# Two pairs of token-major projections by one level of Strassen's product, and x kept in device memory during attention

## The chip, the cores and the metric

The kernel runs on one core of one Trainium2 chip. The core has TensorE (PE, the matmuls; its weight loads are shown apart as PEld), VectorE (DVE), ScalarE (ACT), GpSimd (POOL) and SyncE (SP, which issues most of the DMAs). The metric is device time in microseconds (us), median of runs; a profile is one execution with its own time. Each engine takes its instructions in the order in which the program issues them, and waits on semaphores that the framework puts in.

## The reference, cut to what matters

Two layers over 512 tokens of width 1024. In each layer a normalised and modulated input h goes through one wide projection whose columns are split into thirteen parts; three kinds of attention use them.

```
h = modulate(rms_norm(x, norm1_g), shift1, scale1)
(rq, rk, rv, rg, gq, gk, gv, glr, gg, fq, fk, fv, ff) = split(h @ w_in)     # rv, rg, gv, fv: 512 columns each
ret   = silu(rg) * group_norm(retention(rq, rk, rv))
gla_o = silu(gg) * rms_norm(gla(gq, gk, gv, log_sigmoid(glr @ w_gla_a2 + b) / 16))
fox_o = forgetting_attention(rms_norm(fq), rms_norm(fk), fv, ff + b_fox_f)  # softmax, causal
mixed = sum(sigmoid(h @ w_mg + b_mg) * (branch @ w_br)) @ w_o
x     = x + gate1 * mixed
h2    = modulate(rms_norm(x, norm2_g), shift2, scale2)
x     = x + gate2 * ((silu(causal_dwconv(u)) * g) @ w_down)                 # u, g = split(h2 @ w_up)
```

All of it is float32. The matmuls use float32r, a shorter float32 form, three times: with a = a_hi + a_lo and w = w_hi + w_lo, the product is a_hi w_hi + a_hi w_lo + a_lo w_hi.

## The kernel before

**Data.** Activations are held channel-major: x as eight tiles of 128 channels by 512 tokens, h as eight pairs hhi, hlo. Tiles of 128x512 come from one pool, `slot` (59 buffers). Weights lie in device memory in *units* of 128x1024, in the order of use.

**Weights.** `dma_to` loads unit after unit on SP into a raw buffer (wr, four of them). `prep_hi` (line 118) casts it to the high part wh on ScalarE (L123), `prep_lo` (line 127) makes the low part wl = wr - wh on VectorE (L132). Five buffers hold each of wh and wl. `ahead` (line 247) prepares units up to `depth` ahead of the one in use, four during attention, and one more is loaded; `unit` hands out the next.

**Projections.** `col_block` (line 257) makes 128 output channels for all tokens: one unit, 24 matmuls with 512 columns (8 blocks of channels times three terms, L240 to L242). `tok_group` (line 523) makes a token-major output, four PSUM banks of 128 tokens by up to 512 channels: with 512 channels it takes four units and 8 x 4 x 3 = 96 matmuls (L535 to L537). There are eight PSUM banks: five for projections (`bm`) and three for the attention items (`ba`); `live` counts the latter.

**Attention items and ticks.** The attention's own work is written as generators, *items*: `qk_norm` (norms of the eight fq, fk blocks), `gates_item` and `la_item` (decays of gla and gates of fox), `fox_item` (16 blocks of softmax), `kv_item`, `gla_item`, `ret_item` (16) and, at the end of the last two, `head_out`. Each yields between stages: "e" for engine work, "p" for work that needs PSUM banks, with a condition in some. `tick` (line 205 on) admits the next item from a queue, at most eight at once, not sooner after the one before than the latter's own count of ticks (two for a norm; one, one, two, two for a head's four fox items); it moves every active item by one stage, engine stages first, then pending evacuations, then PSUM stages in order until one does not fit. A column block ticks twice, a unit of a token group twice. So the program order on every engine is a fixed interleaving of projections and items; a stage's instructions wait where they stand, with all that follows on that engine behind them.

**Order in a layer.** After the first group of fq and fk: fv, first half of gq, gk (with ff and glr, 276 columns), second half of gq, gv, four blocks of rq, four of rk, four of gg, rv, four of rg. Rotary blocks are evacuated by `rot_evac` (three VectorE instructions, L690 to L692, and a POOL add, L693). Then the three branches, fox, gla and retention: per branch eight column blocks of w_mg (L870) and four units of w_br. Then w_o, the feed-forward part and w_down, which end in x += gate * out (L907).

**x.** x is in eight buffers of its own for the whole kernel.

Of the kernel before, what the change touches and what calls it, by code (L numbers as in the profile page):

```python
# [52 lines left out]

@with_exitstack
def tile_hybrid_layers(ctx: ExitStack, tc: tile.TileContext, xT, cvec, wall, wada, par, a2, cst, tabs, out):
# [4 lines left out]
    wr_p = ctx.enter_context(tc.tile_pool(name="wr", bufs=4))  # L60
# [40 lines left out]
    crow = const.tile([1, D], F32, tag="crow", name="crow")  # L101
# [3 lines left out]
    x = [const.tile([128, S], F32, tag=f"x{k}", name=f"x{k}") for k in range(KD)]  # L105
# [3 lines left out]
    NU = wall.shape[0]  # L109

    def dma_to(u):
        while state["dma"] < min(u, NU):
            i = state["dma"]
            raw[i] = wr_p.tile([128, UW], F32, tag="wr", name="wr")
            Q.dma_start(out=raw[i], in_=wall[i])
            state["dma"] += 1

    def prep_hi(u):
        while state["prep"] < min(u, NU):
            i = state["prep"]  # L120
            dma_to(i + 1)
            hi = wh_p.tile([128, UW], F32R, tag="wh", name="wh")
            A.copy(hi, raw[i])  # L123
# [3 lines left out]
    def prep_lo(u):  # L127
        while state["lo"] < min(u, NU):
# [3 lines left out]
            V.tensor_tensor(lo, raw.pop(i), hi.bitcast(F32), op=ALU.subtract)  # L132
# [113 lines left out]

    def ahead():
        prep_to(cur[0] + depth[0])
        dma_to(cur[0] + depth[0] + 1)
# [60 lines left out]

    def h_a(l, sec, k, rb, h, ts):
        Acol = mod[l][:, (sec + 1) * 8 + k:(sec + 1) * 8 + k + 1]
        Bcol = mod[l][:, sec * 8 + k:sec * 8 + k + 1]
        t = slot("ht")
# [158 lines left out]
    def layer(l, nm, h):  # L473
# [48 lines left out]

        def tok_group(nunits, kper, width, evac):
# [20 lines left out]

        def v_evac(nm):
            def f(b, o):
                R[nm, b] = slot(nm)
                if b % 2:
                    A.copy(R[nm, b], o)
                else:  # L550
                    V.tensor_copy(R[nm, b], o)
            return f
# [188 lines left out]
        def head_out(br, hh, os, rs, mean, gain, gate):  # L741
            for b in range(NB):
# [9 lines left out]
            yield E_  # L752
            V.scalar_tensor_tensor(out=os, in0=pt, scalar=gain, in1=gate, op0=ALU.mult, op1=ALU.mult)
# [28 lines left out]
        def ret_item(hh, jb):  # L782
# [35 lines left out]
            yield ("e", 0, lambda: [("rg", hh) in R])  # L818
            yield from head_out(0, hh, os, st[:, 8:12], st[:, 0:4], der[l][:, 24 + hh:25 + hh], R["rg", hh])
# [6 lines left out]
        col_block(h, gq_evac(1))  # L826
        R["cos"], R["sin"] = slot("cos"), slot("sin")
# [382 lines left out]
```

## Time and profile before

| | |
|---|---|
| runs before | 1805.62, 1807.52, 1807.56 us; median 1807.52 |
| the profiled execution | 1807.32 us, its span 1805.5 us |
| busy over the span | PE 1796.0, PEld 1503.5, DVE 1001.8, ACT 672.4, POOL 91.0 us |
| weight units prepared (L123, L132) | 302 |
| loads of x | 8 of 256 KB, at the start |
| HBM read, written | 216.44 MB, 2.11 MB |

The span is what the trace covers; the execution's own time is 1.8 us longer. Matmuls are pipelined and their ends modelled, so a busy PE is no proof that it runs at its full pace: the pace is read from counts of matmuls in a stretch. A group's row gives line, engine, operation, tiles written and read, shape and count, then busy us, the mean ns of one, the idle time of the engine just before, and what ended it. The chain of waits is followed backwards from the last instruction: at each step to what released it.

### The profile page before, as it was taken

What the parts mean: (1) busy time and instruction counts of PE and PEld (TensorE: products, weight loads), DVE (VectorE), ACT (ScalarE), POOL (GpSimd) and SP (SyncE); (2) the same over time, 40 slices, a digit from 0 to 9 for tenths busy, and PEclk for the clock granted to TensorE, in tenths of its full rate; (3) what the DMA queues carried; (4) which work ended last, traced back from release to release, by engine and by line L of the source; (5) the groups of instructions that cost most, each with busy time, mean ns of one, the idle gap of its engine ahead of it and who ended that gap; (6) DMA issues with size and microseconds to landing.
All of it is one profiled execution on the core that took longest, in us unless ns stands there. A gap on an engine that the chain in (4) does not pass through costs nothing.

```text
span 1805.5 us, 22557 instructions
## 1 busy us (share of the span) xinstructions
PE 1796.0 (99%) x8991; PEld 1503.5 (83%) x8991; DVE 1001.8 (55%) x1515; ACT 672.4 (37%) x1124; POOL 91.0 (5%) x111
## 2 busy tenths in 40 slices
PE   9999999999999999999999999999999999999999
PEld 6888778888889888888898887888888998888887
DVE  7677654565666776664256576534444466454321
ACT  3674432332324443332138543324223244333220
POOL 3221100000000000000001010000000000000000
PEclk9999999999999999999999999999999999999999
DMA  9332233355543565554223322321322223323231
GB/s 345 120 129 70 71 104 107 129 175 185 177 140 105 183 211 200 197 187 142 81 70 116 119 71 71 117 78 63 104 93 82 82 94 118 104 94 100 70 122 48
DMA packets 64948, 220.03 MB, mean 122 GB/s; under 512 B 7320, under 2 KB 7746, under 8 KB 64843
## 3 DMA queue, kind: packets, MB, share of 16 engines
q1 hardware_dynamic: 64138, 216.47, 36.0%
q0 software_dynamic: 704, 2.11, 0.4%
q8 instruction: 71, 1.16, 0.3%
q14 instruction: 35, 0.28, 0.0%
HBM read 216.44 MB, written 2.11 MB: 121 GB/s over the span
## 4 chain that ended last, share of the span: by engine, by line
PE 93%; DVE 4%; ACT 2%; issue 1%; DMA 0%; SPq 0%; POOL 0%; DVEq 0%; ACTq 0%
PE bm L240 23%; PE bm L242 23%; PE bm L241 23%; PE bm L364 4%; PE ga L364 4%; PE bm L535 3%; PE bm L536 3%; PE bm L537 3%; PE ro L798 1%; PE rs L786 1%; DVE fl L658 1%; ACT wh L123 1%; DVE wl L132 1%; DVE fst L659 1%; DVE fl L656 0%
## 5 line engine op out<-in xcount | busy, mean ns | idle before, releaser
L132 DVE TENSOR_TENSOR wl<-wr,wh 128x1024 fp32r<-128x1024 f32 x302 | 368.7, 1223 | 308.3 <-ACT wh L123 308.0
L240 PE MATMUL bm<-hhi,wh 128*128 128x512 f32 x1296 | 520.3, 401 | 0.0
L242 PE MATMUL bm<-hhi,wl 128*128 128x512 f32 x1296 | 505.5, 390 | 0.0
L241 PE MATMUL bm<-hlo,wh 128*128 128x512 f32 x1296 | 504.9, 390 | 0.0
L123 ACT CAST wh<-wr 128x1024 fp32r<-128x1024 f32 x302 | 314.4, 1046 | 307.0 <-PE bm L241 231.9
L240 PEld LDWEIGHTS bm<-hhi,wh 128*128 128x128 f32 x1296 | 243.5, 188 | 54.2 <-issue 4.2
L241 PEld LDWEIGHTS bm<-hlo,wh 128*128 128x128 f32 x1296 | 243.6, 188 | 53.0 <-issue 2.9
L242 PEld LDWEIGHTS bm<-hhi,wl 128*128 128x128 f32 x1296 | 243.3, 188 | 52.0
L240 PE MATMUL bm<-fah,wh 128*128 128x512 f32 (+1 forms) x374 | 141.0, 377 | 0.0
L241 PE MATMUL bm<-fal,wh 128*128 128x512 f32 (+1 forms) x374 | 140.8, 377 | 0.0
L242 PE MATMUL bm<-fah,wl 128*128 128x512 f32 (+1 forms) x374 | 140.8, 376 | 0.0
L152 DVE SCALAR_TENSOR_TENSOR ar<-ar,cact 128x1024 f32<-128x1024 f32 x80 | 97.4, 1218 | 0.0
L535 PE MATMUL bm<-wh,hhi 128*128 128x512 f32 (+1 forms) x256 | 97.0, 379 | 0.0
L536 PE MATMUL bm<-wl,hhi 128*128 128x512 f32 (+1 forms) x256 | 93.5, 365 | 0.0
L537 PE MATMUL bm<-wh,hlo 128*128 128x512 f32 (+1 forms) x256 | 93.4, 365 | 0.0
L907 DVE SCALAR_TENSOR_TENSOR x<-bm,mod,x 128x512 f32<-128x512 f32 (+1 forms) x39 | 25.5, 655 | 101.3 <-PE bm L242 101.3
L241 PEld LDWEIGHTS bm<-fal,wh 128*128 128x128 f32 x374 | 70.4, 188 | 13.0
L242 PEld LDWEIGHTS bm<-fah,wl 128*128 128x128 f32 x374 | 70.4, 188 | 12.9
L240 PEld LDWEIGHTS bm<-fah,wh 128*128 128x128 f32 x374 | 70.4, 188 | 12.8
L945 DVE TENSOR_TENSOR fu<-fu,bm 128x512 f32<-128x512 f32 x42 | 28.9, 688 | 69.7 <-PE bm L242 59.8
L870 ACT ACTIVATE mg<-bm,der 128x512 f32<-128x512 f32 x48 | 32.9, 685 | 82.4 <-PE bm L242 82.4
L944 ACT ACTIVATE fu<-fu 128x512 f32<-128x512 f32 x44 | 27.8, 633 | 93.7 <-DVE fu L942 93.7
(215 smaller groups left out, 2402.0 us busy)
## 6 DMA issues: line engine op xcount, KB each, us to landing
wr<-wall SPq DMA_DIRECT2D x302, 512.0 KB, 3.5
ar<-wada SPq DMA_DIRECT2D x80, 512.0 KB, 4.0
ad<-wada SPq DMA_DIRECT2D x32, 256.0 KB, 6.1
x<-xT SPq DMA_DIRECT2D x8, 256.0 KB, 4.5
cumb<-cumd POOLq DMA_DIRECT2D x8, 256.0 KB, 4.6
dec<-tabs SPq DMA_DIRECT2D x8, 256.0 KB, 4.2
out<-x SPq DMA_DIRECT2D x8, 256.0 KB, 2.1
cos<-tabs SPq DMA_DIRECT2D x2, 256.0 KB
```

What stands on the lines that cost most here:

```text
L123: A.copy(hi, raw[i])
L132: V.tensor_tensor(lo, raw.pop(i), hi.bitcast(F32), op=ALU.subtract)
L152: V.scalar_tensor_tensor(out=r, in0=r, scalar=1.0, in1=cact, op0=ALU.mult, op1=ALU.mult, accum_out=mod[l][:, b:b + 1])
L240: T.matmul(o, lhsT=wh, rhs=ah, start=first, stop=False)
L241: T.matmul(o, lhsT=wh, rhs=al, start=False, stop=False)
L242: T.matmul(o, lhsT=wl, rhs=ah, start=False, stop=last)
L364: T.matmul(banks[f % GB][:, ts], lhsT=got[f // 8][wi][:, (f % 8) * 128:(f % 8) * 128 + 128], rhs=h[kc][hi][:, ts], start=kc == 0 and hf != ...
L535: T.matmul(o, lhsT=h[k][0][:, bs], rhs=wh[:, ws], start=k == 0, stop=False)
L536: T.matmul(o, lhsT=h[k][0][:, bs], rhs=wl[:, ws], start=False, stop=False)
L537: T.matmul(o, lhsT=h[k][1][:, bs], rhs=wh[:, ws], start=False, stop=k == KD - 1)
L870: A.activation(g, o, AF.Tanh, scale=0.5, bias=der[l][:, i * 8 + j:i * 8 + j + 1])
L945: V.tensor_tensor(t, t, pg, op=ALU.mult)
```

## The change

One level of Strassen's scheme (in Winograd's form with shared sums) is used for two products at a time that share the left operand: fv with gv, and rv with rg. The left operand is h transposed into four quarters (two halves of the tokens, two of the channels), the right one is two weights side by side, cut into the two halves of their channels. Seven products of quarters stand for eight. Sums of quarters of h (ta, tb) are made once per layer by `t_item` from the unsplit h, which `h_a` now keeps, and split into high and low parts. Sums of quarters of the weights are made for each pair on VectorE in the raw buffers, in place, before the split: `_plan` lists the 14 units that a pair prepares from its 8 raw ones, "r" for a raw one, "s" for a sum. So a pair prepares 14 units for 8, and a unit of a pair serves 12 matmuls.

rg, before made channel-major in four column blocks, comes out token-major, so retention's gate is multiplied in `head_out` ahead of the transposes. The order in the layer becomes gk, gq, gq, pair fv and gv, pair rv and rg, rq, rk, gg; fox items wait for fv. Two loops in `pair_group` run ticks alone until a condition holds. Three more units are loaded ahead instead of one, into six raw buffers.

x becomes eight tiles of the slot pool (65 buffers), which are free during attention: x is read again from device memory ahead of the third branch, in layer 1 from a copy that layer 0 writes by POOL's queue after w_down. crow becomes two tiles of the pool.

```diff
+def _plan():
+    def pair():
+        a11, a21, a22, a12 = ((b + 2 * i, b + 2 * i + 1) for i in range(4))
+        for i in range(2): v.append(("r", a11[i]))
+        for i in range(2): v.append(("s", a21[i], a21[i], a22[i], ALU.add))
+        for i in range(2): v.append(("s", a11[i], a21[i], a11[i], ALU.subtract))
+        for i in range(2): v.append(("r", a12[i]))
+        for i in range(2): v.append(("s", a12[i], a12[i], a11[i], ALU.subtract))
+        for i in range(2): v.append(("s", a11[i], a22[i], a11[i], ALU.subtract))
+        for i in range(2): v.append(("r", a22[i]))
...
-    wr_p = ctx.enter_context(tc.tile_pool(name="wr", bufs=4))
+    wr_p = ctx.enter_context(tc.tile_pool(name="wr", bufs=6))
...
-    x = [const.tile([128, S], F32, tag=f"x{k}", name=f"x{k}") for k in range(KD)]
+    x = [slot("x") for _ in range(KD)]
...
     def prep_hi(u):
         while state["prep"] < min(u, NU):
             i = state["prep"]
             dma_to(i + 1)
+            p = plan[i]
+            if p[0] == "s":
+                prep_lo(i - 1)
+                V.tensor_tensor(raw[p[1]], raw[p[2]], raw[p[3]], op=p[4])
             hi = wh_p.tile([128, UW], F32R, tag="wh", name="wh")
-            A.copy(hi, raw[i])
+            A.copy(hi, raw[p[1]])
...
     def ahead():
         prep_to(cur[0] + depth[0])
-        dma_to(cur[0] + depth[0] + 1)
+        dma_to(cur[0] + depth[0] + far[0])
...
+        def t_item(k):
+            yield E_
+            ...
+            V.tensor_tensor(ta[:, H0], c[:, H1], c[:, H0], op=ALU.subtract)
+            V.scalar_tensor_tensor(out=ta[:, H1], ...)
+            V.scalar_tensor_tensor(out=tb[:, H0], ...)
+            V.scalar_tensor_tensor(out=tb[:, H1], ...)
+            yield E_
+            A.copy(ah, ta)
+            A.copy(bh, tb)
+            yield E_
+            V.tensor_tensor(al, ta, ah.bitcast(F32), op=ALU.subtract)
+            V.tensor_tensor(bl, tb, bh.bitcast(F32), op=ALU.subtract)
+            tt[k, 1], tt[k, 2] = (ah, al, 0), (ah, al, 256)
+            tt[k, 3], tt[k, 4] = (bh, bl, 0), (bh, bl, 256)
+
+        def pair_group(done):
+            flush()
+            while live[0] > NA - 1:
+                tick()
+            ...
+            bA, bB = [bm(), bm()], [bm(), bm()]
+            o11, o12, o21, o22 = ([slot("pr"), slot("pr")] for _ in range(4))
+            def prod(banks, key, first, evac):
+                ahead()
+                us = [unit()]
+                ahead()
+                us.append(unit())
+                for t in range(2):
+                    for k in range(4):
+                        ...
+                        T.matmul(banks[t], lhsT=ah[:, ts], rhs=wh[:, ws], start=first and k == 0, stop=False, ...)
+                        T.matmul(banks[t], lhsT=ah[:, ts], rhs=wl[:, ws], start=False, stop=False, ...)
+                        T.matmul(banks[t], lhsT=al[:, ts], rhs=wh[:, ws], start=False, stop=k == 3, ...)
+                        if k == 1:
+                            tick()
+                    pend.append(lambda t=t: evac(t))
+                    tick(1, False)
+
+            prod(bA, 11, True, lambda t: A.copy(o11[t], bA[t]))
+            while len(tt) < 16:
+                tick()
+            prod(bB, 1, True, lambda t: A.copy(o22[t], bB[t]))
+            prod(bA, 2, False, lambda t: A.copy(o12[t], bA[t]))
+            while live[0] > NA - 1:
+                tick()
+            bC = [bm(), ba()]
+            ...
+            prod(bC, 21, True, e11)
+            prod(bB, 22, False, lambda t: V.tensor_tensor(o12[t], o12[t], bB[t], op=ALU.add))
+            prod(bA, 3, False, lambda t: V.tensor_tensor(o22[t], o22[t], bA[t], op=ALU.add))
+            ...
+            prod(bA, 4, False, e21)
...
-            yield ("p", 1, lambda: [("qn", hh) in R, ("qn", 4 + hh) in R, "cumb" in R])
+            yield ("p", 1, lambda: [("qn", hh) in R, ("qn", 4 + hh) in R, "cumb" in R, ("fv", NB - 1) in R])
...
                     V.tensor_scalar(o, o, mean[:, b:b + 1], rs[:, b:b + 1], op0=ALU.add, op1=ALU.mult)
+                    V.tensor_tensor(o, o, gate[b][:, hh * 128:hh * 128 + 128], op=ALU.mult)
...
-        tok_group(4, 2, 512, v_evac("fv"))
+        for k in range(4):
+            queue.append((t_item(k), 1))
+        far[0] = 3
+        tok_group(3, 3, GKW, gk_evac)
         col_block(h, gq_evac(0))
-        tok_group(3, 3, GKW, gk_evac)
         col_block(h, gq_evac(1))
+        pair_group(fg_done)
...
-        tok_group(4, 2, 512, v_evac("gv"))
+        pair_group(r_done)
+        far[0] = 1
         for i in range(4):
             col_block(h, rot_evac("rq", i))
...
-        tok_group(4, 2, 512, v_evac("rv"))
-        for i in range(4):
-            col_block(h, gate_evac("rg", i))
...
             if bi == 2:
+                for k in range(KD):
+                    x[k] = slot("x")
+                    Q.dma_start(out=x[k], in_=xT[k * 128:k * 128 + 128, :] if l == 0 else xs[k])
...
+        def upd5(j, o, ts=FULL):
+            upd5x(j, o, ts)
+            if l < L - 1:
+                ...
+                G.dma_start(out=xs[j][:, ts], in_=x[j][:, ts])
...
-NSLOT = 59
+NSLOT = 65
```

More of the change, by code (lines that the diff above doesn't have):

```diff
@@ L51, with plain @@
 NC = _o
+H0 = slice(0, S // 2)
+H1 = slice(S // 2, S)
+def _plan():
+    v, w = [], [0]
+    def plain(n):
+        for _ in range(n):
+            v.append(("r", w[0]))
+            w[0] += 1
+    def pair():
+        b = w[0]
+        a11, a21, a22, a12 = ((b + 2 * i, b + 2 * i + 1) for i in range(4))
+        for i in range(2):
+            v.append(("r", a11[i]))
+        for i in range(2):
+            v.append(("s", a21[i], a21[i], a22[i], ALU.add))
+        for i in range(2):
+            v.append(("s", a11[i], a21[i], a11[i], ALU.subtract))
+        for i in range(2):
+            v.append(("r", a12[i]))
+        for i in range(2):
+            v.append(("s", a12[i], a12[i], a11[i], ALU.subtract))
+        for i in range(2):
+            v.append(("s", a11[i], a22[i], a11[i], ALU.subtract))
+        for i in range(2):
+            v.append(("r", a22[i]))
+        w[0] += 8
+    for _ in range(L):
+        plain(8 + 3 + 2)
+        pair()
+        pair()
+        plain(12 + 36 + 8 + 6 + 2 * (KFF - 3) + KFF)
+    lim, m = [0], 0
+    for t in v:
+        m = max([m] + [i + 1 for i in t[1:4] if isinstance(i, int)])
+        lim.append(m)
+    return v, lim
 @with_exitstack
@@ L104, in tile_hybrid_layers @@
     warm = const.tile([128, S], BF16, tag="warm", name="warm")
-    x = [const.tile([128, S], F32, tag=f"x{k}", name=f"x{k}") for k in range(KD)]
+    x = [slot("x") for _ in range(KD)]
     state = {"prep": 0, "lo": 0, "dma": 0}
     raw, wgt = {}, {}
-    NU = wall.shape[0]
+    plan, wlim = _plan()
+    NU = len(plan)
     def dma_to(u):
-        while state["dma"] < min(u, NU):
+        while state["dma"] < wlim[min(u, NU)]:
             i = state["dma"]
@@ L131, in prep_lo @@
             lo = wl_p.tile([128, UW], F32R, tag="wl", name="wl")
-            V.tensor_tensor(lo, raw.pop(i), hi.bitcast(F32), op=ALU.subtract)
+            V.tensor_tensor(lo, raw[plan[i][1]], hi.bitcast(F32), op=ALU.subtract)
             wgt[i] = (hi, lo)
@@ L752, in head_out @@
             yield E_
+            if mean is not None:
+                R["br", br, hh] = split(pt, "ob", gain)
+                free()
+                return
             V.scalar_tensor_tensor(out=os, in0=pt, scalar=gain, in1=gate, op0=ALU.mult, op1=ALU.mult)
@@ L829, in layer @@
         Q.dma_start(out=R["sin"], in_=tabs[1])
-        tok_group(4, 2, 512, v_evac("gv"))
+        pair_group(r_done)
+        tt.clear()
+        far[0] = 1
         for i in range(4):
             col_block(h, rot_evac("rq", i))
-        for p in range(2):
-            for half in range(2):
-                queue.append((kv_item(p, half), 1))
         for i in range(4):
             col_block(h, rot_evac("rk", i))
+        for hh in range(NH):
+            R["dec", hh] = slot("dec")
+            Q.dma_start(out=R["dec", hh], in_=tabs[2 + hh])
+        for hh in range(NH):
+            for jb in range(NB):
+                queue.append((ret_item(hh, jb), 1))
         for i in range(4):
@@ L841, in layer @@
             queue.append((gla_item(hh), 2))
-        tok_group(4, 2, 512, v_evac("rv"))
-        for hh in range(NH):
-            R["dec", hh] = slot("dec")
-            Q.dma_start(out=R["dec", hh], in_=tabs[2 + hh])
-        for i in range(4):
-            col_block(h, gate_evac("rg", i))
-        for hh in range(NH):
-            for jb in range(NB):
-                queue.append((ret_item(hh, jb), 1))
         ada_on[0] = True
@@ L1013, in tile_hybrid_layers @@
         V.tensor_copy(onesr, ones)
-        Q.dma_start(out=crow, in_=cvec)
+        crow = [slot("crow") for _ in range(2)]
+        for i in range(2):
+            Q.dma_start(out=crow[i][0:1, :], in_=cvec[:, i * S:i * S + S])
         for k in range(KD):
@@ L1030, in tile_hybrid_layers @@
         for i in range(2):
-            T.matmul(pc[i], lhsT=ones[0:1, :], rhs=crow[0:1, i * S:i * S + S], start=True, stop=True)
+            T.matmul(pc[i], lhsT=ones[0:1, :], rhs=crow[i][0:1, :], start=True, stop=True)
         heat(W0)
```

89 lines of the change are left out of this document (70 added, 19 removed).

## The prediction

> **What bounds the kernel now.** I read the page's busy times and its chain first, then the stages, then the layer's attention stretch in order of time. Columns of a stage: stretch, its length, busy time (instructions) of PE, PEld, DVE, ACT, POOL, granted clock, DMA share, GB/s.
>
> ```profile
> PE 1796.0 (99%) x8991; PEld 1503.5 (83%) x8991; DVE 1001.8 (55%) x1515; ACT 672.4 (37%) x1124; POOL 91.0 (5%) x111
> PE 93%; DVE 4%; ACT 2%; issue 1%; DMA 0%; SPq 0%; POOL 0%; DVEq 0%; ACTq 0%
> ...
> 400.00:500.00 100.00, 100.00 (x443) 82.81 (x442) 59.78 (x82) 28.49 (x36) 0.00 (x0) 1.00 0.52 174
> ...
> 60.00:110.00 50.00, 49.98 (x262) 42.77 (x261) 34.49 (x41) 40.24 (x66) 9.06 (x7) 1.00 0.38 126
> 160.00:210.00 50.00, 50.00 (x246) 40.66 (x246) 38.59 (x65) 19.97 (x42) 7.93 (x7) 1.00 0.23 74
> ```
>
> TensorE sets the end: 93% of the chain. From 400 to 500 us it runs only 512-column matmuls, 443 in 100 us, so one costs 0.2257 us, and a unit of 24 (a column block) 5.42 us. But the same rows warn: where attention runs beside the projections, VectorE is 77% busy (160 to 210) and ScalarE 80% (60 to 110). The chain there, in order of time (start, length, what):
>
> ```profile
> 118.70 1.92 PE la L616 x8
> 130.27 0.86 PE laS L630 x4
> 131.13 0.79 PE lan L635 x8
> 158.28 0.89 PE fo L678 x8
> ...
> 168.34 0.69 DVE rt L690
> 170.73 1.30 DVE fl L658
> 172.87 0.94 ACT wh L123
> 173.83 1.22 DVE wl L132
> ...
> 207.53 0.69 DVE rt L690
> ```
>
> Between 168 and 208 us the chain leaves PE for VectorE and ScalarE. One rotary block starts each (207.53 - 168.34)/5 = 7.84 us, not 5.42. Forgetting attention's own PE work in these 2.42 us: 80 fo matmuls at 0.89/8 = 0.11 are 8.9 us, the 72 of fs and fT at about the same price 8; some 17 to 18 us over ten blocks, 1.8 a block. So 0.6 us a block, 6 us a layer, is already stall. VectorE is nearly the bound here before anything is added.
>
> **The change, part by part.** *Saved matmuls.* Per layer fv, gv, rv (96 each) and rg (four blocks of 24, 96) are 384 matmuls; two pairs of 7 products, each 2 x 4 x 3 = 24, are 336. 48 x 0.2257 = 10.8 us a layer, 21.7 in all. This stands if PE stays the bound.
>
> *What VectorE gets.* Its rows over the first layer's attention stretch, and two more shapes (line, shapes, count | busy us, mean ns | idle before, releaser):
>
> ```profile
> L132 DVE TENSOR_TENSOR wl<-wr,wh 128x1024 fp32r<-128x1024 f32 x37 | 45.0, 1220 | 23.7 <-ACT wh L123 23.6
> L467 DVE TENSOR_TENSOR qsl<-qsq,qsh 128x512 fp32r<-128x512 f32 x8 | 10.3, 1292 | 12.7 <-ACT qsh L466 12.7
> L658 DVE TENSOR_TENSOR fl<-fl,cst 128x128 f32<-128x128 f32 x16 | 9.2, 577 | 0.5
> L656 DVE SCALAR_TENSOR_TENSOR fl<-fs,cumc,cumb 128x128 f32<-128x128 f32 (+3 forms) x16 | 8.7, 542 | 5.3 <-PE fs L652 3.5 <-DMA cumb<-cumd 1.9
> L659 DVE TENSOR_REDUCE fst<-fl 128x1 f32<-128x128 f32 (+3 forms) x16 | 7.8, 487 | 0.5
> L496 DVE SCALAR_TENSOR_TENSOR qy<-qsq,qy 128x512 f32<-128x512 f32 x8 | 5.4, 679 | 0.0
> L736 DVE SCALAR_TENSOR_TENSOR st<-st,an,kv 128x128 f32<-128x128 f32 x14 | 4.9, 348 | 3.0 <-PE kv L721 2.3
> L467 DVE TENSOR_TENSOR fbl<-fo,fbh 128x512 fp32r<-128x512 f32 x4 | 2.7, 685 | 1.8 <-ACT fbh L466 1.8
> L663 DVE RECIPROCAL fst<-fst 128x1 f32<-128x1 f32 x16 | 2.5, 155 | 0.8 <-ACT fl L661 0.8
> L626 DVE TENSOR_TENSOR la<-la,lae 128x512 f32<-128x512 f32 x2 | 1.3, 671 | 0.0
> ...
> L315 DVE SCALAR_TENSOR_TENSOR ht<-x,mod,rb 128x256 f32<-128x256 f32 x16 | 7.6, 480 | 2.3 <-ACT rb L306 2.3
> ...
> L123 ACT CAST wh<-wr 128x1024 fp32r<-128x1024 f32 x37 | 38.4, 1046 | 0.0
> ```
>
> A pair loads the same 8 raw units but prepares 14: six more splits (1.22 on VectorE, 1.05 on ScalarE), and eight of them are first summed by a VectorE instruction of L132's shape, 1.22 us. A product of two summed units costs VectorE 4 x 1.22 = 4.9 us against 5.42 us of PE. And `prep_hi`/`prep_lo` issue sum, cast, low part one behind the other: the low part waits for ScalarE's cast of what VectorE has just summed, so 1.05 us more passes idle per summed unit, 7.0 us a product. Before, the cast needed nothing from VectorE and ran ahead.
>
> ```profile
> DVE wl L132 <- ACT wh L123: 308.0, 184, 5.4
> ...
> 167.01 1.23 DVE L132 TENSOR_TENSOR wl<-wr,wh 128x1024 fp32r<-128x1024 f32 x1 [1.83 <-ACT wh L123]
> ```
>
> Here VectorE stands still in front of exactly this instruction (308 us in the span, once 1.83 us under load), with its later work queued behind it. The Trainium skill ("TensorE: Matmul & The Clock Gate", on queue depths in the part on the array) has VectorE and ScalarE as strict FIFO. By that the 1.05 us are lost in full; if later instructions could pass, each layer would be 16 us cheaper than my sum. These two rows agree with the page.
>
> *Where it falls.* Work items enter one by one at ticks. Of layer 0, three gk units and two gq blocks give 2 ticks each, the first product 4: 14. Eight norms enter at every second tick, so the four t items (`t_item`) enter at ticks 17 to 20 and end at 22: the loop that waits for them runs 8 ticks with no product between. In layer 1 two blocks come first, the t items enter at 15 to 18, and 2 ticks are run so. Fox items now wait for fv, so all 16 run in pair B (24 of its 28 ticks), kv behind them. The last product accumulates into bA, which VectorE must have read one product before; so PE cannot end pair B before VectorE has come through its sixth product. VectorE's work from the start of pair A to there, layer 0: low parts of 26 units 31.7 (three of pair A's are issued earlier, one of rq comes in), 15 sums 18.3, t items 4 x (4 x 0.48 + 2 x 0.68) = 13.1, norms not yet finished, about four at 1.29 + 0.68 + 0.75 = 11, decay (6 x 0.67) and gates (seven instructions, about as much) 8, fox 30.9 less 4.6, kv 16 x 0.35 = 5.6, evacuations 12 x 0.69 = 8.3. The 4.6: L658 takes 0.29 alone and 1.30 beside POOL's rotary add, which no longer runs then:
>
> ```profile
> 130.16 0.29 DVE L658 TENSOR_TENSOR fl<-fl,cst 128x128 f32<-128x128 f32 x1
> ...
> L945 DVE TENSOR_TENSOR fu<-fu,bm 128x512 f32<-128x512 f32 x42 | 28.9, 688 | 69.7 <-PE bm L242 59.8 <-ACT fu L944 9.9
> ```
>
> (L945 is the row for an evacuation that adds.) Sum 122, and 15 waits of 1.05 make 138 us. In layer 1 two norms are left, 133. PE in the same stretch: 324 matmuls 73.1, fox 18, decay 1.92 + 2 x (0.86 + 0.79) = 5.2, gates, kv and norms 5: 101 us, 100 in layer 1. Stall: 37 and 33 us.
>
> *Bounds.* If the cast waits cost nothing, 16 a layer less. If each product takes the longer of VectorE and PE with no carry between them (low parts are issued two products ahead, 3 to 19 us of VectorE per product), it comes to 9 a layer more. I take the sum: evacuations tie the engines closely, but two products of look-ahead carry something.
>
> *Given back.* Rotary blocks without fox run at 5.42: 6 us a layer.
>
> *Edits at little or nothing.* Retention's gate is multiplied token-major: four 128-wide VectorE instructions more per head, about 4.4 us a layer, and gla's heads now share the stage of the mg blocks. VectorE there was 53% busy:
>
> ```profile
> 260.00:291.00 31.00, 31.00 (x140) 25.24 (x139) 16.56 (x24) 11.38 (x21) 1.01 (x1) 1.00 0.27 85
> ...
> x<-xT SPq DMA_DIRECT2D x8, 256.0 KB, 4.5
> wr<-wall SPq DMA_DIRECT2D x302, 512.0 KB, 3.5
> ```
>
> Some 18 us more in about 65 make 80%, where fox's stage lost 0.6 us a block: 0 to 7 a layer, I take 2. The eight reloads of x are issued on SP ahead of the third branch, twelve units (65 us) before their first reader, and land in 4.5 us; uncovered, or with the weight loads stuck behind them, 5 us a layer. The stores of x go by POOL's queue in a stage where POOL does nothing (0.00 in the row of 400 to 500). crow in two parts, tabd and the slots: 0 to 1 us, taken as 0.
>
> **The sum**, against the profiled execution's own 1807.3 us (span 1805.5; it lies 0.2 below the runs' median 1807.5): layer 0 -10.8 + 37 - 6 = +20, layer 1 -10.8 + 33 - 6 = +16, mg stages +4. 1807 + 40 = **1847 us**.
>
> **The rivals.** *PE stays the bound* (the other side). If the look-ahead of four units and VectorE's idle 45% took up the sums, the saved matmuls would be seen: 1807.3 - 21.7 = 1786, and up to 12 less for the fox stage. For it: the page's share. Against: the idle time lies in other stages. It decides itself at the row of pair A: only if a summed product costs VectorE less than 5.42 us, which with an idle cast it does not (7.0). Halfway, the casts are free and only VectorE's busy time counts: stalls 21 and 17, the sum 1847 - 32 = 1815, and with the old stalls gone entirely (9 a layer) about 1803.
>
> *The clock falls.* In the wait loops PE idles for the first time since the start. What an idle PE does, the start shows:
>
> ```profile
> 13.16 2.15 PE warm L1027 x5
> ...
> 17.03 3.07 PE warm L1027 x10
> 20.10 0.68 PE ga L364 x3
> ```
>
> 0.43 us a matmul, then 0.31, then 0.227 as work goes on, though the clock column says 1.00. Three idle stretches a layer (loop, first and sixth product of pair B), 15 matmuls each at 0.43: 3 us x 6, so 1865. At worst all of both pairs: 324 at 0.43 plus 28 is 167 against 138 and 133, some 63 more, 1910. Against it: in DVE-bound products a slow PE is partly hidden, and gaps of 1 to 3 us are short. The Trainium skill (same page, "Part 1: The HAM clock gate") lets the clock go to half after an idle window of about 3.4 us and back after a busy one; by that only the loops and pair B's first product would pay. This trace has no such gap after the start.
>
> *Raw buffers.* Six hold what eight units of a pair need; a12 is loaded only when a21 is read for the last time, and the next pair's a22 when this one's low part is made, three low parts (3.7 us) before it is summed, against 3.5 us of landing. If each of four such places were late by a landing: +14, 1861.
>
> **How the numbers follow.** My forecast, VectorE's sums bound the pairs (1815 to 1870): 0.65. PE stays the bound or nearly (1775 to 1803): 0.13. Clock or buffers (above 1860): 0.18; that gain and loss cancel (1804 to 1811), 0.04. The range from 1803 to 1878 takes in the free-cast bound and most of the clock case. 0.2%, 3.6 us, is about what a measurement can tell. Faster 0.13, same 0.04, slower 0.83.
>
> **What would show it.** Right: PE's count of 512-column matmuls down by 96; in pair A and B VectorE above 85% busy or idle only before wl on ScalarE; PE's idle time in front of the products after the t items, ending on tal or tah; the chain through wr, wl and fl; rotary blocks at 5.42. Wrong: PE back to back at 0.2257 through both pairs, or a stall that ends on wr's DMA or on SP.

## The result, and the profile after

The changed kernel takes 1911.61 us (median of 4 runs, 1910.10 to 1912.86) against 1806.64 us before (4 runs beside it, 1805.62 to 1807.56): ratio 1.058, 95% interval [1.0562, 1.0599], 105 us slower. The forecast was 1847 us with a range up to 1878: the direction is right, the size is not.

The page of the changed kernel: busy times, the chain by engine, and the two groups that prepare weight units.

```profile
span 1911.1 us, 22671 instructions
...
PE 1820.6 (95%) x8895; PEld 1506.8 (79%) x8895; DVE 1092.1 (57%) x1657; ACT 716.9 (38%) x1184; POOL 108.9 (6%) x120
...
PE 85%; DVE 7%; ACT 4%; issue 2%; DMA 0%; POOL 0%; SPq 0%; ACTq 0%; DVEq 0%; POOLq 0%
...
L179 DVE TENSOR_TENSOR wl<-wr,wh 128x1024 fp32r<-128x1024 f32 x326 | 396.7, 1222 | 314.9 <-ACT wh L170 305.7
L170 ACT CAST wh<-wr 128x1024 fp32r<-128x1024 f32 x326 | 338.8, 1047 | 437.1 <-PE bm L288 271.2
```

PE has the 96 instructions less that seven products for eight promise (8991 to 8895), and 24 more units are prepared (302 to 326). TensorE's share of the chain falls from 93% to 85%; VectorE, ScalarE and issue take it.

The stages of the changed kernel (columns as in the prediction), cut at the first matmuls of the pairs: pair A and pair B of layer 0, then of layer 1, then the stretch from the first evacuation of the mg blocks to the end.

```profile
89.70:180.30 90.60, 63.74 (x217) 46.31 (x216) 64.01 (x82) 45.20 (x70) 9.30 (x10) 0.74 0.20 64
180.30:269.30 89.00, 74.05 (x386) 55.52 (x385) 56.63 (x111) 44.91 (x91) 0.00 (x0) 0.92 0.21 65
1039.80:1122.30 82.50, 58.05 (x214) 43.76 (x213) 58.68 (x76) 38.46 (x58) 6.63 (x8) 0.81 0.21 70
1122.30:1211.30 89.00, 74.01 (x386) 55.51 (x385) 56.59 (x111) 44.91 (x91) 0.00 (x0) 0.92 0.20 65
...
1293.60:1911.00 617.40, 613.29 (x2991) 516.06 (x2989) 275.90 (x376) 198.60 (x314) 10.24 (x9) 1.00 0.28 92
```

The two pairs last 179.6 and 171.5 us; the prediction had 138 and 133. That is 42 + 38 = 80 us, more than the whole 65 us that it missed by; 15 come back elsewhere, 5 of them in the last row here (below). The amount of VectorE's work was right: 64.01 + 56.63 = 120.6 us in layer 0, against 122 predicted, and its larger terms were near too (sums 18.2 us for 18.3, fox 26.0 for 26.3). But VectorE is only 71% and 64% busy in the two pairs. It isn't full, and neither is TensorE. What fills the difference is waiting between engines, seen in the waits of layer 0's pairs (who waited for whom: us in total, times, longest):

```profile
DVE wl L179 <- ACT wh L170: 27.0, 19, 2.8
ACT wh L170 <- DVE wr L168: 20.8, 11, 2.6
...
PEld qn L541 <- ACT qsh L522: 10.6, 4, 4.6
DVE fbl L523 <- ACT fbh L522: 10.3, 2, 8.1
...
DVE qsl L523 <- ACT qsh L522: 6.7, 4, 2.5
...
DVE fst L795 <- ACT fl L793: 4.3, 6, 0.8
```

The first two rows are the ping-pong of the weight sums: the cast waits for the sum, the low part for the cast. In this view no engine waits for a weight load. The others are items: a norm (qsl, qn) and a fox block (fbl, fst). A norm's way through the engines stands in the chain of waits of the changed kernel, from the end of pair A's first product into the loop that waits for the t items (start, length, what):

```profile
99.21 0.53 ACT qsq L536
...
101.44 0.63 ACT qsq L548
102.07 0.52 ACT qsh L522
...
102.61 1.37 DVE qsl L523
...
104.03 0.81 PE qn L542
...
104.86 0.69 ACT qy L545
...
107.84 1.37 DVE qsl L523
...
112.83 1.36 DVE qsl L523
```

From ScalarE to VectorE to PE and back to ScalarE: qsl starts at 102.61, 107.84 and 112.83, one norm after another every 5.1 us. Beside the first of these two steps PE has the last six matmuls of the first product, beside the second no product at all: that loop lasts from 107.3 to 118.1 us. In the kernel before, the same instruction, five times:

```profile
L467 DVE TENSOR_TENSOR qsl<-qsq,qsh x5: 1375/1379/1385, 87.2 to 108.1; 128x512 fp32r<-128x512 f32 x5
```

(108.1 - 87.2)/4 = 5.2 us. This pace is that of the matmuls, which have no gap there (PE 49.98 of 50 us in the prediction's row from 60 to 110): one norm comes every two ticks, and two ticks of a unit with 24 matmuls held 5.42 us of them, enough to hide a norm. A product of a pair has four ticks in 5.42 us, so two ticks hold only 2.71 us. The lengths of the chain's pieces could be read in the trace of before, though not its pace.

### The profile page after: what moved, and what is told of

It is laid out like the page before. It is cut to its first block, busy times and chain, and to the rows that moved or that the text cites. A ratio compares the mean times of both kernels' runs of the same rounds, so it can differ in the third digit from the quotient of the medians.

```text
span 1911.1 us, 22671 instructions
## 1 busy us (share of the span) xinstructions
PE 1820.6 (95%) x8895; PEld 1506.8 (79%) x8895; DVE 1092.1 (57%) x1657; ACT 716.9 (38%) x1184; POOL 108.9 (6%) x120
## 4 chain that ended last, share of the span: by engine, by line
PE 85%; DVE 7%; ACT 4%; issue 2%; DMA 0%; POOL 0%; SPq 0%; ACTq 0%; DVEq 0%; POOLq 0%
PE bm L287 22%; PE bm L289 22%; PE bm L288 22%; PE bm L420 4%; PE ga L420 4%; ACT wh L170 1%; PE bm L628 1%; PE bm L632 1%; PE bm L630 1%; DVE wr L168 1%; DVE wl L179 1%; PE ro L935 1%; PE rs L923 1%; DVE fl L788 1%; PE fo L810 1%
## 5 line engine op out<-in xcount | busy, mean ns | idle before, releaser
L179 DVE TENSOR_TENSOR wl<-wr,wh 128x1024 fp32r<-128x1024 f32 x326 | 396.7, 1222 | 314.9 <-ACT wh L170 305.7
L170 ACT CAST wh<-wr 128x1024 fp32r<-128x1024 f32 x326 | 338.8, 1047 | 437.1 <-PE bm L288 271.2
L287 PE MATMUL bm<-hhi,wh 128*128 128x512 f32 x1232 | 488.5, 396 | 0.0
L289 PE MATMUL bm<-hhi,wl 128*128 128x512 f32 x1232 | 479.9, 390 | 0.0
L288 PE MATMUL bm<-hlo,wh 128*128 128x512 f32 x1232 | 479.6, 389 | 0.0
L287 PEld LDWEIGHTS bm<-hhi,wh 128*128 128x128 f32 x1232 | 231.3, 188 | 50.7 <-issue 2.9
L288 PEld LDWEIGHTS bm<-hlo,wh 128*128 128x128 f32 x1232 | 231.4, 188 | 50.1 <-issue 1.9
L288 PEld LDWEIGHTS bm<-fal,wh 128*128 128x128 f32 x374 | 70.4, 188 | 12.8
L289 PEld LDWEIGHTS bm<-fah,wl 128*128 128x128 f32 x374 | 70.4, 188 | 12.8
L287 PE MATMUL bm<-mxh,wh 128*128 128x256 f32 (+1 forms) x176 | 58.6, 333 | 0.0
L289 PE MATMUL bm<-mxh,wl 128*128 128x256 f32 (+1 forms) x176 | 58.3, 331 | 0.0
L288 PE MATMUL bm<-mxl,wh 128*128 128x256 f32 (+1 forms) x176 | 58.3, 331 | 0.0
```

What stands on the lines that cost most here:

```text
L170: A.copy(hi, raw[p[1]])
L179: V.tensor_tensor(lo, raw[plan[i][1]], hi.bitcast(F32), op=ALU.subtract)
L287: T.matmul(o, lhsT=wh, rhs=ah, start=first, stop=False)
L288: T.matmul(o, lhsT=wh, rhs=al, start=False, stop=False)
L289: T.matmul(o, lhsT=wl, rhs=ah, start=False, stop=last)
```

## The experiments

All are timed against the kernel before on the same chip. "Ratio" is to that kernel, with its 95% interval.

**Everything but the seven products** (e1_plain): the order, x in device memory, six raw buffers and token-major gates of the changed kernel, with plain token groups; no weight sums, t items or wait loops, and two ticks a unit.

```diff
-        pair()
-        pair()
+        plain(16)
...
-        pair_group(fg_done)
+        tok_group(4, 2, 512, keep("fv"))
+        tok_group(4, 2, 512, keep("gv", ...))
```

> The order of the changed kernel (gk, gq, fv, gv, rv, rg, then rq, rk, gg; rg token-major; x read again), with the plain eight products: no sums, no t items, no wait loops. If Strassen's own work on VectorE and its hand-offs cost the time, this stands near the kernel before: 1802 to 1820. If the new order alone costs it (fox held back until fv is done, norms in a bunch), 1850 or more.

Measured 1807.66 us, ratio 1.001 [0.9999, 1.0022]. The whole loss belongs to what this kernel leaves out: the products with their sums, t items, loops and ticks.

**The sums one unit early** (e2_sum_ahead): VectorE makes the next sum while ScalarE casts the last.

```diff
...
+            sum_of(i)
             A.copy(hi, raw[p[1]])
+            sum_of(i + 1)
```

> Each weight sum is issued one unit earlier, so that VectorE makes the next sum while ScalarE casts this one. VectorE's amount of work is unchanged. Theory amount (the sum of VectorE's busy time decides): no more than 5 us faster, 1906 to 1912. Theory hand-offs (VectorE stands idle behind ScalarE's cast, 1.05 us at each of 32 sums): 20 to 34 us faster, 1878 to 1892.

Measured 1880.54 us, ratio 1.041 [1.0383, 1.0444]: 31 us less. The prediction priced the cast waits at 16 us a layer, 32 in all. In the waits of layer 0's pairs VectorE's idle time in front of low parts falls from 27.0 to 17.0 us.

**No wait loop** (e3_t_first): the t items at the head of the queue.

```diff
-            queue.append((t_item(k), 1))
+            queue.insert(k, (t_item(k), 1))
```

> The four t items go to the head of the queue instead of behind the norms; VectorE does the same work, but the loop that ticks without products runs no more. Theory amount: within 8 us of the changed kernel. Theory hand-offs (in the loop the norms' chains ScalarE, VectorE, PE, ScalarE, POOL, VectorE run one after the other with nothing beside them): pair A shrinks by 20 to 35 us in layer 0 and 10 to 15 in layer 1, 1862 to 1882, and the clock stays at 1.00 there.

Measured 1910.51 us, ratio 1.058 [1.0549, 1.061]. The loop goes and nothing is gained, as was expected had VectorE's amount of work set the time. But the norms that ran in the loop now run in the products: five of their qsl start between 94.42 and 123.76 us, 5.2 to 10.5 us apart, so the products still wait for norms.

**Fox after the pairs** (e4_fox_late): fox items wait until pair B is done.

```diff
-            yield ("p", 1, lambda: [..., "cumb" in R, ("fv", NB - 1) in R])
+            yield ("p", 1, lambda: [..., "cumb" in R, "rg" in R])
```

> Fox items wait for the second pair, so they run beside the rotary blocks as before the change. If fox beside the sums is what makes pair B 89 us long: pair B 45 to 55, rotary blocks 7.5 to 8 instead of 5.4, in all 15 to 25 us a layer faster, 1862 to 1882. If pair B is bound by the sums and casts themselves: pair B stays above 65 and the time above 1890.

Measured 1889.6 us, ratio 1.046 [1.0433, 1.0494]. The stages of this run, pair A and pair B of layer 0:

```profile
87.50:173.50 86.00, 58.86 (x217) 42.74 (x216) 63.93 (x82) 45.13 (x70) 9.31 (x10) 0.78 0.20 68
173.50:213.30 39.80, 38.50 (x170) 31.44 (x169) 27.16 (x27) 19.33 (x23) 0.00 (x0) 1.00 0.43 143
```

Pair B, now almost without items, takes 39.8 us for seven products, 5.69 each, with every sum and cast wait in it and PE busy for 38.5. So sums alone don't bound a pair: with fox items in it, it took 89.0. Pair B is 49 us shorter in each layer, but the kernel only 22 us in all: fox goes back beside the rotary blocks and behind (from the first to the last evacuation of layer 0's mg blocks it is 218 us for 200).

**No sums** (e5_no_sums: the raw quarters go into the products as they are), and **half the ticks** (e6_sparse: as without the loop, and two ticks per product instead of four, the density of before), then **both cures** (e7_sparse_ahead) and **half the ticks without sums** (e15_sparse_no_sums).

```diff
 # e5, e15
-            if p[0] == "s":
-                prep_lo(i - 1)
-                V.tensor_tensor(raw[p[1]], raw[p[2]], raw[p[3]], op=p[4])
 # e6, e7, e15
-                    tick(1, False)
```

> Leaves out the 32 sums of weights (the raw quarters go into the seven products instead), all else as in the changed kernel. VectorE is rid of 32 x 1.22 = 39 us and of the waits behind the casts. Theory amount: all 39 us and the waits' 34 are seen, 1838 to 1850. Theory hand-offs: most of what the sums cost was the wait, which the run with the sums one unit earlier has gained already; little more than that run, 1865 to 1878.

> The t items at the head of the queue, and two ticks per product of a pair in place of four, so that a tick has 2.7 us of products beside it as in a column block. Same work on every engine. Theory density (an item's chain through ScalarE, VectorE, PE and POOL takes some 5 us for two ticks, whatever PE does): pair A 50 to 60, pair B 50 to 65 us, rotary blocks above 5.42 again; 1835 to 1865. Theory amount: 1900 to 1912, as the run with t items first.

> As the run with two ticks per product, and each weight sum issued one unit earlier. Theory density and hand-offs: 15 to 30 us below that run, 1812 to 1845, pair A near 45. Theory amount: no more than 5 us below it.

> Two ticks per product instead of four, and the 32 weight sums left out (their products take a cast quarter instead, so the output is not the reference's). Two ticks alone gave 1882, two ticks with the sums early 1850. If VectorE's amount of work is what is left with the sums early, leaving the sums out takes it away as well: about 1815. If what is left are the chains between engines, the time stays near that with the sums early: 1840 to 1850.

Together they make a table (us, median; ratios: 1.031 [1.0278, 1.0338] for e5, 1.041 [1.0383, 1.0443] for e6, 1.023 [1.0204, 1.0263] for e7, 1.0145 [1.0128, 1.0161] for e15):

| | sums in place | sums one unit early | no sums |
|---|---|---|---|
| four ticks a product | 1911.6 | 1880.5 | 1863.0 |
| two ticks a product | 1882.0 | 1849.6 | 1832.7 |

The second row also has the t items first, which alone was worth 1 us in the first column; in the other columns it was not run alone. The columns and rows add up: early sums are worth 31 and 32 us, the sums' own work 18 and 17, the ticks 30, 31 and 30. From 1911.6 the three take 79 us; the last cell is still 26 us above the kernel before, though 21.7 us of matmuls are gone. The ticks are worth less than was expected of them: two ticks alone were to give 1835 to 1865 us, and 1812 to 1845 with early sums. The last cell lies between the 1815 expected had VectorE's amount been what was left, and the 1840 to 1850 for the chains. The stages of the last cell and of the one left of it, pair A and pair B of layer 0 (no sums, then early sums):

```profile
94.00:148.90 54.90, 48.73 (x198) 36.88 (x197) 43.99 (x48) 42.57 (x66) 12.20 (x12) 0.94 0.28 90
148.90:211.60 62.70, 58.52 (x280) 45.33 (x279) 39.24 (x72) 36.28 (x72) 0.01 (x1) 1.00 0.30 99
```

```profile
92.90:152.60 59.70, 52.02 (x198) 38.56 (x197) 54.35 (x57) 43.02 (x66) 12.42 (x12) 0.89 0.27 85
152.60:218.50 65.90, 59.88 (x281) 46.61 (x280) 45.04 (x77) 36.29 (x72) 0.00 (x0) 0.97 0.30 99
```

With early sums VectorE is 91% busy in pair A (54.35 of 59.70): there its work is near the bound, as the prediction had it for all of both pairs.

**The density alone, in the kernel before** (e8_before_dense): four ticks per unit of a 512-wide token group instead of two (two behind each half of the unit), nothing of the change.

```diff
+                    if width == 512 and kk:
+                        tick()
...
+                        if width == 512:
+                            tick(1, False)
```

> The kernel before, with nothing of the change but four ticks per unit in the token groups of fv, gv and rv (as dense as in the pairs, twice as dense as before). Theory density: eight norms of about 5 us run against 27 us of products, so 10 us or more of stall a layer, and more where fox meets gv: 1825 to 1850, with the clock below 1.00 there. Theory amount: no change, 1803 to 1811.

Measured 1842.72 us, ratio 1.020 [1.0166, 1.0225]: 35 us lost without one sum. From 60 to 120 us PE is busy for 51.5 us, before for 60.0, and no other engine is full there (VectorE 38.5 us, ScalarE 43.5). The norms run one behind the other (VectorE's last two of eight):

```profile
96.07 1.36 DVE L467 TENSOR_TENSOR qsl<-qsq,qsh 128x512 fp32r<-128x512 f32 x1 [1.05 <-ACT qsh L466]
...
101.01 1.37 DVE L467 TENSOR_TENSOR qsl<-qsq,qsh 128x512 fp32r<-128x512 f32 x1 [2.19 <-ACT qsh L466]
```

From 71.36 us on, six steps of 4.94 us each: with 2.71 us of matmuls to two ticks, the chain sets this pace. This run and the table's rows show a cause that the prediction lacked.

**A warm TensorE** (e10_heat): the changed kernel with matmuls of no use, 12 per tick in the wait loop and one per block of channels in the first two products of each pair.

```diff
+                for _ in range(12):
+                    T.matmul(bB[0], lhsT=warm[:, 0:128], rhs=warm, start=True, stop=True)
```

> The changed kernel with matmuls put in that compute nothing (a bank that is overwritten later): 12 behind each tick of the wait loop, one behind each block of the first two products of each pair, so that PE is never idle long. Theory clock (PE at half speed in the pairs is what costs): the clock stays at 1.00 and most of the 64 us beyond the prediction come back, 1850 to 1875. Theory density: only the matmuls that ran at 0.43 us are gained, at most 17 us, less what the added ones cost, 1893 to 1912.

Measured 1909.97 us, ratio 1.057 [1.054, 1.0601]. Two stages of the changed kernel, then of this run (the column before the last two is the granted clock):

```profile
120.00:150.00 30.00, 20.19 (x65) 14.79 (x65) 23.40 (x36) 14.92 (x23) 2.94 (x5) 0.57 0.19 60
...
180.00:225.00 45.00, 35.87 (x159) 26.53 (x158) 26.41 (x56) 24.09 (x55) 0.00 (x0) 0.89 0.11 36
```

```profile
120.00:150.00 30.00, 28.19 (x130) 17.57 (x131) 23.93 (x37) 15.08 (x24) 2.94 (x5) 0.94 0.18 58
...
180.00:225.00 45.00, 36.42 (x173) 24.53 (x175) 27.57 (x58) 24.83 (x57) 0.00 (x0) 1.00 0.11 36
```

The clock rises from 0.57 to 0.94 and from 0.89 to 1.00, and VectorE gets as much done in the same time as before: the slow clock looks like a mark of the stall and not its cause. This isn't shown to the end: the added matmuls take time of PE too, so a gain of the clock that they just eat up can't be excluded.

**Other places for the items**, on top of both cures: fox held until pair B is done (e11_fox_late), the rotary query blocks ahead of pair A (e12_rq_first), and that with fox admitted from the middle of pair B (e13_rq_fox_mid).

```diff
 # e11
-            yield ("p", 1, lambda: [..., ("fv", NB - 1) in R])
+            yield ("p", 1, lambda: [..., "rg" in R])
 # e12: ahead of pair_group(fg_done)
+        for i in range(4):
+            col_block(h, rot_evac("rq", i))
```

> T items first, two ticks per product, sums one unit earlier, and fox items held until the second pair is done. Theory density: pair B about 40 us instead of 65, rotary blocks 7.5 to 8 instead of 6, fox ends later and may leave a wait ahead of its branch: 1820 to 1842 against the run without the last edit (1850). Theory amount: 1847 to 1853.

> T items first, two ticks per product, sums one unit earlier, and the four rq blocks ahead of the first pair, so that the norms have 22 us more of plain products beside them. Theory density: pair A falls from 60 to 42-48 us in both layers, the rq blocks run at 5.4 to 6; pair B as before at 60-65: 1818 to 1835. If pair A's length came from the sums and not from the norms: pair A stays above 55 and the time at 1845 or more.

> As the run with the rq blocks first, and fox items admitted only from the fourth product of pair B on, so that the rest of them falls beside rk and gg. Theory density: pair B 45 to 55 us, rk and gg blocks 7 to 8: 1805 to 1825; a gain over the kernel before (1806) only if no tick runs without products. Theory amount: as the run with the rq blocks first.

Measured 1859.4 us (1.029 [1.0261, 1.032]), 1867.2 (1.033 [1.0304, 1.0364]) and 1870.06 (1.035 [1.032, 1.038]): all above the 1849.6 they began from, where the expectations had 1805 to 1842. Fox taken from a pair is late where it goes: the mg blocks of layer 0, from the first evacuation to the last, take 218 and 221 us in the two runs that hold it back, and 200 without. With the rotary blocks first, pair A takes 63.5 us in layer 0 (42 to 48 expected); its norms still run to 148 us, and POOL's adds come beside the sums (told at the end), so it doesn't tell norms from sums.

**One pair** (e14_one_pair; its lines below are against the kernel before): the order of before, only rv and rg as a pair at rv's place, early sums, two ticks a product. Three runs then moved items around it: the t items queued ahead of gv (e18_t_early), that and gla's output items behind the pair (e17_t_early_gla_late), the same with the t items ahead of rq (e19_t_rq_gla_late). Last, the second of these with the t items at the head of the queue (e20_t_head).

```diff
-        tok_group(4, 2, 512, v_evac("rv"))
-        for i in range(4):
-            col_block(h, gate_evac("rg", i))
+        pair_group(r_done)
 # e17, e19, e20
         pair_group(r_done)
+        for hh in range(NH):
+            queue.append((gla_item(hh), 2))
 # e20, after the first rq block
+                    queue.insert(k, (t_item(k), 1))
```

> Only the pair with the values and the router gate's weights (rv with rg) by seven half products, at the place of the old value groups; queries and keys as before with four ticks of items in a unit; the weight sums one unit early, two ticks per product. The pair's seven products have about 5.4 us less of TensorE's work a layer than the eight. If the loss comes from items whose chain of engines lasts longer than the product that hides it, this pair, with few items left for it, should run near TensorE's pace: 1800 to 1812 us. If VectorE's sums are themselves the bound of a pair, the pair costs some 20 us a layer as the second pair does now: 1840 to 1850.

> The one-pair kernel (1819) with its four t items queued ahead of the value group of the second branch instead of behind the rotary query blocks, so that they are done long before the pair. In the one-pair kernel TensorE idles and runs slow for about 10 us more than before around the pair's first product (225 to 250 us of layer 0), while the state updates of the second branch wait behind the t items on VectorE. If that crowding is the loss, this gives 1799 to 1808; if the loss is the second branch's own chain, it stays at 1815 to 1820.

> As the run with early t items, and the four output items of the second branch queued behind the pair instead of ahead of it, so that nearly no item runs within the pair. If chains of items in a pair are what makes a product longer than its matmuls, the pair then runs at 5.5 us a product and the time is 1795 to 1803, below the kernel before; if the items only move their loss to the blocks behind the pair, 1806 to 1815.

> As the last, but with the t items queued just ahead of the rotary query blocks, one group later. If where the t items run doesn't matter once they are out of the way of the state updates, the same time as the last run within 4 us; if the norms of the first 100 us are crowded by early t items, this one is the faster by 4 to 8 us.

> The kernel with one pair, early t items and the second branch's output items behind the pair (1818), with its t items put at the head of the queue after the first rotary query block: in that kernel they stood behind the items of the third branch and so still ran at 221 to 234 us, where the state updates of the second branch wait behind them on VectorE. Its products 1 to 4 already take 5.4 us each, the length of their matmuls; what is left is the stretch around the first product (12.8 us instead of 5.4, and some 6 us of waits and slow matmuls ahead of it). If the t items' crowd is the cause, 1798 to 1806, at or below the kernel before (1806); if the state updates are late by themselves, 1812 to 1818.

Measured 1819.11 us (1.007 [1.0055, 1.0085]), 1817.28 (1.006 [1.0048, 1.0074]), 1818.25 (1.0065 [1.0053, 1.0078]), 1818.39 (1.006 [1.005, 1.0078]) and 1827.87 (1.011 [1.0096, 1.0132]). In the three middle runs the t items ran at about the same place as in the first, since they still stood behind the fox items in the queue: these runs tested only gla's items. The first of the five was expected at 1800 to 1812, and the one with gla's items behind the pair at 1795 to 1815: both are slower than that. The pair in the run with gla's items behind it, layer 0, first product and the other six:

```profile
236.40:249.20 12.80, 10.60 (x58) 7.51 (x57) 7.89 (x13) 2.69 (x3) 0.00 (x0) 0.75 0.25 83
249.20:282.50 33.30, 33.02 (x146) 26.96 (x145) 23.25 (x27) 15.86 (x18) 0.00 (x0) 1.00 0.52 171
```

Six products take 33.3 us, 5.55 each, PE busy throughout, and VectorE 70%: the half products with their sums do run at TensorE's pace. The first one takes 12.8, and ahead of it PE waits (layer 0 of the same run, in order of time):

```profile
232.92 0.68 DVE L610 TENSOR_TENSOR tal<-ta,tah 128x512 fp32r<-128x512 f32 x1
...
234.50 1.12 DVE L876 SCALAR_TENSOR_TENSOR st<-st,an,kv 128x128 f32<-128x128 f32 x3
235.38 1.12 PE L861 MATMUL kv<-gv,lae 64*64 64x128 f32 x12 [3.70 <-DVE st L876]
```

The state updates of gla wait on VectorE behind the t items' low parts, and PE behind them. The last run took the t items away from there, and became slower still: fox and rotary blocks are late then (the last fs at 229.6 us instead of 206.3, the last rt at 214.5 instead of 207.8). Its row from 180 to 200 us, and the same row of the kernel before:

```profile
180.00:200.00 20.00, 17.11 (x77) 13.87 (x78) 15.76 (x26) 7.35 (x15) 2.97 (x3) 0.91 0.23 80
```

```profile
180.00:200.00 20.00, 20.00 (x103) 16.45 (x102) 14.57 (x24) 8.63 (x18) 2.58 (x2) 1.00 0.21 59
```

I expected 1798 to 1806 from it, had the crowd at that place been the loss: that theory fell. One pair saves 24 matmuls, 5.4 us a layer, and in none of five arrangements does that pay for its t items and sums.

## Why the prediction was right in direction and wrong in size

- **Saved matmuls, 10.8 us a layer**: right as a count (96 fewer), and never seen in the time.
- **VectorE's work in the pairs, 122 us**: right (120.6).
- **Cast waits**: 27.0 us of idle time in layer 0 for the 16 predicted, but what they cost, by the runs that make sums early, is 31 and 32 us for both layers: the sum had 32. Early sums are worth 16 us a layer and take only 10 of these 27.0 away: the amount is right, but this idle time isn't all of it.
- **"Sum 122, and 15 waits of 1.05 make 138 us"**: this step failed. It takes the stretch for VectorE's busy time plus one kind of wait. VectorE stood idle for 179.6 - 120.6 = 59 us of layer 0's pairs: 27.0 in front of low parts, and 21 in front of three instructions of items (fbl 10.3, qsl 6.7, fst 4.3), which the sum puts at nothing. "Where it falls" counted at which tick an item enters, and not how long its chain of engines lasts from one item to the next (4.9 to 5.2 us a norm) against the matmuls that cover it (2.71 us). The density of ticks is worth 30 us by three pairs of runs, and 35 us in the kernel before by itself: some half of the 65 us that the forecast missed by. The other half is not assigned (below).
- **"Two products of look-ahead carry something"**, and the rival's point of decision, **7.0 us a summed product**: look-ahead carries more than that; a pair without items has 5.69 a product in spite of the sums. The rival's mechanism is real in such a pair, but in this kernel the pairs are where the items are.
- **Wait loops**: predicted as the place of PE's idle time. In part they were (107.3 to 118.1 us in layer 0; PE idles 26.9 us in all of its pair A), but taking them out is worth nothing (1910.5).
- **The clock**: it fell as that rival said, to 0.57 in a stage of pair A and 0.74 in all of it. The price that the rival gave to it isn't seen: with the clock back at 0.94 the time is the same, and 35 us are lost in the kernel before with denser ticks at a mean clock of 0.995. Its worst case, 1910 us, lies next to the measured 1911.6 by chance: it has both pairs at half the clock throughout, and they had 0.74 to 0.92. The Trainium skill ("TensorE: Matmul & The Clock Gate", "Part 1: The HAM clock gate") has the clock fall after an idle window of TensorE of about 3.4 us. The rows agree only in part, since shorter waits did it too. In pair A's first product, where the prediction, by that rule, expected no slow matmul, they start 0.42 to 0.43 us apart behind waits of 0.97 and 0.90 us:

```profile
92.19 0.49 PE L541 MATMUL qn<-qsh,onesr 128*128 128x512 f32 x1 [0.97 <-ACT qsh L522]
93.58 0.50 PE L542 MATMUL qn<-qsl,onesr 128*128 128x512 f32 x1 [0.90 <-DVE qsl L523]
...
94.82 0.63 PE L628 MATMUL bm<-wh,hhi 128*128 128x512 f32 x1
95.24 0.63 PE L630 MATMUL bm<-wl,hhi 128*128 128x512 f32 x1
```

- **Raw buffers**: no wait on a weight load shows in layer 0's pairs.
- **Given back**: rotary blocks run at 5.4 as predicted, the eight of layer 0 from 275.8 to 313.7 us (VectorE's first instruction of two blocks in a row, changed kernel):

```profile
302.12 0.69 DVE L822 TENSOR_TENSOR rt<-bm,sin 64x512 f32<-64x512 f32 x1 [2.21 <-PE bm L289]
...
307.56 0.69 DVE L822 TENSOR_TENSOR rt<-bm,sin 64x512 f32<-64x512 f32 x1 [2.21 <-PE bm L289]
```

- **The mg stages, +4 for two layers**: not so. From the first evacuation there to the end layer 1 has 617.4 us, 3 us less than before where 2 more were forecast. The run with everything but the products has 617.5 there, so this comes with the order and not with the products. Before (same cut):

```profile
1184.80:1805.00 620.20, 616.99 (x2974) 519.38 (x2972) 268.93 (x351) 196.08 (x301) 6.46 (x6) 1.00 0.27 90
```

- **x in device memory, the order, token-major gates at nothing**: right, 1807.66 with all of these.
- **The lower end of the range, about 1803**: its working doesn't come out. The 9 us a layer of old stalls stand in no row; taken off in full they give 1797, and less the 6 that the sum has already given back, 1809. The result doesn't rest on it.

The loss, by the table: the change loses 105 + 21.7 = 127 us besides what it saves. 31 are the sums' hand-over, 17 their work, 30 the ticks. The last cell's 26 and the 21.7 saved, 48, stay. In the cell without sums and with half the ticks the pairs of layer 0 last 54.9 + 62.7 = 117.6 us for the 101 of PE's work that the prediction had counted; VectorE again waits at norms and fox blocks, and no run took these out of the pairs without putting them in another's way. PE's own idle time there is 10 us, 6.3 of it in front of matmuls of the pairs' last products, into banks that VectorE had still to read (pr): the tie that the prediction named. Part of it shows only behind the pairs: against the run with everything but the products, layer 0 of the last cell is 8 us late at its first rotary block (223.8 for 215.5) and 14 at its first mg evacuation (307.8 for 294.2). How the 48 split between t items, norms and fox stays open, and so does what it costs that a pair's fourth product takes one of the items' three PSUM banks (bC): no run gave it back.

## What to carry to other kernels

The length of a stretch in which several engines hand work to each other need not be the busiest engine's busy time: take one item's chain of engines from one admission to the next, and compare it with the work that lies between the two ticks. Whoever makes a loop body's work shorter, or its ticks denser, takes cover away from all that runs in it; the time per tick belongs in the prediction. And work saved on the engine that bounds the kernel is only saved if the stretch was bound by it in each part, and if what the saving needs elsewhere can start before it is wanted: sums one unit earlier were worth 31 us.

## What the runs showed of the hardware that was not expected

VectorE instructions with two inputs get held when POOL runs a tensor add or product, and POOL's when VectorE runs one of these. The run with rotary query blocks first, VectorE and then POOL, in order of time:

```profile
106.50 0.69 DVE L533 TENSOR_TENSOR qsl<-qsq,qsh 128x512 fp32r<-128x512 f32 x1
107.11 2.32 DVE L167 TENSOR_TENSOR wr<-wr 128x1024 f32<-128x1024 f32 x1
109.35 2.31 DVE L189 TENSOR_TENSOR wl<-wr,wh 128x1024 fp32r<-128x1024 f32 x1
```

```profile
106.72 1.62 POOL L834 TENSOR_TENSOR rq<-rq,rt 128x512 f32<-128x512 f32 x1 [5.34 <-PE bm L299]
108.31 2.27 POOL L559 TENSOR_TENSOR qsq<-qsq,qv 128x512 f32<-128x512 f32 x1
```

A sum and a low part take 2.3 us each for 1.22, and POOL's product 2.27 us. The same product in layer 0's pairs of the changed kernel (group of five, mean in ns):

```profile
L549 POOL TENSOR_TENSOR qsq<-qsq,qv 128x512 f32<-128x512 f32 x5 | 6.4, 1272 | 27.0 <-ACT qsq L548 27.0
```

So both engines pay. In the last one-pair run a subtraction of 128x128 on VectorE, 0.29 us alone, takes as long as POOL's add beside it:

```profile
216.22 1.31 DVE L798 TENSOR_TENSOR fl<-fl,cst 128x128 f32<-128x128 f32 x1
```

```profile
216.10 1.28 POOL L833 TENSOR_TENSOR rk<-rk,rt 128x512 f32<-128x512 f32 x1 [7.33 <-DVE rk L832]
```

A norm's chain holds this too. Its qsl takes 1.36 us in the rows above, beside a product on POOL, where fbl of the same line and shape takes 0.69 in the prediction's row; so some 0.7 of a norm's 5 us are POOL's:

```profile
102.15 1.27 POOL L549 TENSOR_TENSOR qsq<-qsq,qv 128x512 f32<-128x512 f32 x1 [9.17 <-ACT qsq L548]
```

The prediction had met this for one instruction alone (L658), and not for the sums. The Trainium skill ("GPSIMD Engine Reference", "1. Specifications") says that GpSimd shares its SBUF interfaces with VectorE's instructions that have two inputs there; these rows agree, and give the price.
